# Norms of a one-layer hybrid decoder step: the sums of squares taken as columns of tokens, the last norm read from PSUM

## The chip, the cores and the metric

The kernel runs on one core of one Trainium2 chip. The metric is the device time of one execution in microseconds (us). Before the change it is 2406.41 us, the median of three runs (2404.97 to 2407.44).

## The reference, cut to what matters

One layer of a decoder with 512 prompt tokens and 32 sample tokens (eight sequences of four), D_MODEL = 2048, D_FF = 5632, all in float32:

```
def rmsnorm(x, w):
    y = xf * lax.rsqrt(jnp.mean(xf * xf, axis=-1, keepdims=True) + EPS)
    return (y * w.astype(jnp.float32)).astype(x.dtype)
...
h = rmsnorm(x, norm_mix_w);  proj = h @ w_in
...                                   # differential attention, and a Mamba-2 scan
y = y * jax.nn.silu(z)
y = rmsnorm(y.reshape(b, s, SSD_GROUPS, D_SSD // SSD_GROUPS), ...)
x = x + jnp.concatenate([att, y], axis=-1) @ w_out
hf = rmsnorm(x, norm_ffn_w);  g = hf @ w_gate;  u = hf @ w_up
...                                   # causal conv of width 3 on g
x = x + (jax.nn.silu(g_c) * u) @ w_down
y_prompt = rmsnorm(xp, norm_final_w);  y_sample = rmsnorm(xs, norm_final_w)
```

The norms that matter here are the first one, one for each of the two groups of the scan's output, the one ahead of the gated MLP, and the last one. There is also a small norm for each attention head, which the change leaves as it is.

## The kernel before, in words

Activations lie with features on the 128 partitions and tokens along the free dimension: 544 tokens in two halves of 272 (`HT`; in each half 256 prompt and 16 sample tokens). Weights stream from HBM in tiles of 128x1024, and each is split into a high and a low part (`whi` by ScalarE, `wlo` by VectorE), so that a product is three passes of TensorE over 272 columns (`mm3`, line 166). These products write the tiles `po`; there are nearly twelve thousand of them in the projections alone, and they fill the kernel.

TensorE's instructions run in exactly the order in which the code issues them. The other engines are put in order by a scheduler, except for a short stretch at the start of the MLP where the code's order holds for them too. Side work (attention, the scan, norms) consists of Python generators held by the class `Side` (line 61). After each `mm3` the generators whose time has come are resumed; `yield 5.0` asks to be resumed when TensorE has been given 5 us of further work by the planner's count. `side.finish(cond)` (line 89) doesn't wait for that count: it resumes generators at once until the condition holds, and puts no products in between.

A sum of squares over 2048 (or 512) features is built as a tile `sq` of 128x544 by ScalarE and VectorE or GpSimd. The sum over the partitions is a product with a 128x128 tile of ones, which leaves the same sum on every partition: one float32 product per half, 272 columns wide, into a tile `pn` (line 212). In the trace each float32 product is two instructions. ScalarE takes the square root of 128x272 values from `pn`, VectorE the reciprocal.

The places of these norms, by the names that the rest of the text uses:

- **norm1**: the first norm, at `k == 13` of the first products (line 281, helper `rms_rstd`, line 207). The following `podt` products and the evacuations of `xbc` use it.
- **gate0**: the norm of group 0 of the scan (line 622). It comes in the middle of the second `ssd` generator, ahead of the last small products of that generator, `pys` (line 598). Then `mixy[0]` is scaled and written to DRAM (`mixd`, line 626), and so is `mixy[1]` (`yd`, line 683). After it the pool `sS` is released. The first tiles of the next pool, `sT`, wait for every earlier user of that memory: the copy `q<-po` (line 728) waits for all these DMAs, and TensorE waits for the copy, which frees its `po` buffers.
- **gate1**: the norm of group 1 (line 1046), at the start of the output projection.
- **scaled**: a first scale of the residual for the MLP's input, from two of its sixteen tiles (line 1204).
- **norm2**: the norm ahead of the MLP (line 1315). Its result replaces the scale from `scaled`; the first evacuation of the gate branch asks for it by `side.finish` (line 303).
- **final0**, **final1**: the last norm, for each half of the tokens (`final`, line 1469). Half 0 runs beside the last products of half 1. Half 1 is the end of the kernel: 16 products of 128x272 on VectorE (10) and GpSimd (6), and the writes of `yT`.

The constants come in packs (`PACKS`, line 49). Each is one DMA.

Of the kernel before, what the change touches and what calls it, by code (L numbers as in the profile page):

```python
# [9 lines left out]
F32 = mybir.dt.float32  # L10
# [6 lines left out]
P = 128  # L17
# [31 lines left out]
PACKS = {  # L49
    "k0": [("nw_mix", P, NK), ("epsc", P, 1)],  # L50
    "k1": [("ones", P, P), ("nw_ffn", P, NK), ("nw_fin", P, NK)],
    "kS": [("conv_ssd", P, NC_X * (CW + 1)), ("prev_ssd", P, NC_X * DB * 3), ("dt_bias", P, SH), ("a_log", P, SH),
           ("d_skip", P, 8), ("maskT", P, P), ("tri", P, P), ("tri32", NS, NS3), ("blk32", NS, NS3),
           ("mask32", NS, NS), ("bmask", NS3, DB), ("ii", 2 * SH, SH), ("ii32", 2 * NS, NS), ("w_dt", P, NK * SH)],
    "kT": [("ident", P, P), ("nw_ssd", P, 8), ("cos", P, TOK), ("sin", P, TOK), ("cmask", P, P), ("smask", P, NS), ("sel", P, 64), ("isel", P, 64),
           ("csgn", P, 2), ("hmask", P, 2), ("dmask", P, 8), ("subw", P, 1), ("lamv", 64, 4)],
# [43 lines left out]
def body(tc, i, o):  # L100
# [105 lines left out]

    def rms_rstd(pool, sq, n, **kw):

        r = pool.tile([P, 2, HT], F32, name="rstd", **kw)
        for hf in range(2):  # L210
            pt = ps.tile([P, 512], F32, name="pn", tag=("sA", "pb")[hf])
            mm(pt[:, 0:HT], ones, sq[:, hf, :])
            A.activation(r[:, hf], pt[:, 0:HT], AF.Sqrt, scale=1.0 / n, bias=epsc)
            V.reciprocal(r[:, hf], r[:, hf])
        return r


    k0 = pack(cst, "k0")
    nw_mix, epsc = k0["nw_mix"], k0["epsc"]
    sK = tc.alloc_tile_pool(name="sK", bufs=1)  # L220
    kT = {}
    sC = tc.alloc_tile_pool(name="sC", bufs=1)
    sA = tc.alloc_tile_pool(name="sA", bufs=1)
    xs = {}
# [37 lines left out]
    k1 = pack(cst, "k1")  # L262
    ones, nw_ffn, nw_fin = (k1[n] for n in ("ones", "nw_ffn", "nw_fin"))
    V.tensor_tensor(ssq, ssq, ssq2, op=ALU.add)
    kS = pack(sC, "kS")
    kT.update(pack(sK, "kT"))
    ident, nssd = kT["ident"], kT["nw_ssd"]
    cpar = kS["conv_ssd"].rearrange("p (j t) -> p j t", t=CW + 1)
# [7 lines left out]
    for k in range(NK):  # L276
        for f in range(2):
            for hf in range(2):
                mm3(first[f][hf], kslice(fw[f], k), xs[k], hf, k == 0, k == NK - 1)
        if k == 13:  # L280
            rstd = rms_rstd(cst, ssq, DM, tag="rstd")
    sA.release()
# [335 lines left out]
    def gate0():  # L618
        my = mixy[0]
        while not squared:  # L620
            yield 0.7
        r = rms_rstd(sS, sq, 512, tag="spre", bufs=2)
        with tc.high_priority(offset=60):
            for j in range(4):
                V.scalar_tensor_tensor(my[:, j], my[:, j], nssd[:, j:j + 1], r, op0=ALU.mult, op1=ALU.mult)
                dma(out=mixd[8 + j], in_=my[:, j])
# [417 lines left out]
    def gate1():  # L1044
        yield 3.5
        rg = rms_rstd(sT, sq, 512, tag="pss")
        for j in range(4):
            n = 10 + j
            V.scalar_tensor_tensor(ys[j], ys[j], nssd[:, 4 + j:5 + j], rg, op0=ALU.mult, op1=ALU.mult)
            ms[n] = xslot(n)  # L1050
            A.activation(ms[n][0], ys[j], AF.Copy)
            V.tensor_tensor(ms[n][1], ys[j], rd(ms[n][0]), op=ALU.subtract)
# [149 lines left out]
    def scaled(x, s):  # L1202
        yield 6.5
        scale.append(rms_rstd(cst, ssq, 2 * P, tag="rstd"))
        for m in range(2):
            feed(m, x[m])
# [304 lines left out]
def host_inputs(x):  # L1511
# [132 lines left out]
```

## Time and profile before

| | |
|---|---|
| median of three runs | 2406.41 us |
| profiled execution, its own time | 2406.29 us |
| span in that profile (first to last instruction) | 2404.5 us |
| TensorE busy | 2342.6 us, 97% |
| VectorE busy | 1961.7 us, 82% |
| mean granted TensorE clock | 0.989 of full speed |

The profile comes from one execution. What an execution takes beyond its span (2406.29 - 2404.5 = 1.8 us) lies around the first and the last instruction. The share of busy time says which engine is used most; what a place costs is read from the idle time of TensorE there, and from what ended it.

### The profile page before, as it was taken

The numbers are of one execution on the slowest core, as the hardware profiler recorded it, in microseconds if no ns is written. First come the engines' busy times: TensorE is split into PE (matmuls) and PEld (weight loads), VectorE is DVE, ScalarE is ACT, GpSimd is POOL, SyncE is SP. The second block draws the span as 40 slices with busy tenths as digits, with TensorE's granted clock in tenths as the row PEclk, the third lists the DMA queues.
The fourth block names the chain that finished last, engine by engine and source line by source line (L and its number), as shares of the span: only waits on it lengthen the run. The fifth ranks groups of instructions, "written<-read, shape, count | busy, mean of one in ns | idle before, by whom it ended". The sixth has DMA issues, their size and how long they took to land.

```text
span 2404.5 us, 46378 instructions
## 1 busy us (share of the span) xinstructions
PE 2342.6 (97%) x18184; PEld 2294.0 (95%) x18184; DVE 1961.7 (82%) x2677; ACT 1200.5 (50%) x1917; POOL 612.4 (25%) x619
## 2 busy tenths in 40 slices
PE   7999989999999999999999999999999999999997
PEld 7999989999999999999999999999999899999996
DVE  8686779887877556988988888898888978878876
ACT  5645336666575333554444445444444644545455
POOL 4253233332321111222222222222221111211213
PEclk9999999999999999999999999999999999999998
DMA  4444444545454443334334343433433755747432
GB/s 159 133 125 140 147 161 145 165 151 165 160 170 151 157 140 118 123 124 139 119 123 135 110 141 125 140 118 121 136 110 132 225 183 178 231 154 253 122 123 75
DMA packets 172285, 350.44 MB, mean 146 GB/s; under 512 B 19474, under 2 KB 89874, under 8 KB 172066
## 3 DMA queue, kind: packets, MB, share of 16 engines
q1 hardware_dynamic: 168370, 335.51, 44.0%
q0 software_dynamic: 2880, 11.14, 1.1%
q8 instruction: 142, 2.33, 0.4%
q10 hardware_dynamic: 816, 0.84, 0.1%
q14 instruction: 77, 0.63, 0.1%
HBM read 293.07 MB, written 54.35 MB: 144 GB/s over the span
## 4 chain that ended last, share of the span: by engine, by line
PE 83%; DVE 9%; DMA 3%; issue 3%; ACT 2%; POOL 0%; SPq 0%; DVEq 0%; ACTq 0%; POOLq 0%
PE po L158 76%; PE scs L158 1%; DMA st<-hTs 1%; DVE xl L1083 1%; DVE wlo L1083 1%; PE pos L158 1%; DVE wx L1083 1%; PE sc L158 1%; DMA wraw<-in_w_last 1%; DVE wlo L151 1%; PE pys L158 1%; PE pvo L158 1%; PE py L158 0%; DMA xr<-in_xT 0%; DVE ssq L1501 0%
## 5 line engine op out<-in xcount | busy, mean ns | idle before, releaser
L158 PE MATMUL po<-xh,whi 128*128 128x272 f32 x3968 | 1158.1, 292 | 17.6 <-DVE q L728 6.3
L158 PE MATMUL po<-xh,wlo 128*128 128x272 f32 x3968 | 1150.1, 290 | 7.6 <-DVE wlo L151 4.3
L158 PE MATMUL po<-xl,whi 128*128 128x272 f32 x3968 | 1149.2, 290 | 4.7 <-DVE xl L254 4.5
L158 PEld LDWEIGHTS po<-xh,whi 128*128 128x128 f32 x3968 | 755.0, 190 | 25.8 <-issue 10.2
L158 PEld LDWEIGHTS po<-xh,wlo 128*128 128x128 f32 x3968 | 753.3, 190 | 14.5 <-DVE wlo L151 6.2
L158 PEld LDWEIGHTS po<-xl,whi 128*128 128x128 f32 x3968 | 754.0, 190 | 6.2 <-DVE xl L254 5.8
L1083 DVE TENSOR_TENSOR wlo<-wx,whi 128x1024 fp32r<-128x1024 f32 (+2 forms) x340 | 423.6, 1247 | 96.8 <-ACT whi L1089 94.2
L1089 ACT ACTIVATE whi<-wx 128x1024 fp32r<-128x1024 f32 (+2 forms) x340 | 342.1, 1006 | 293.0 <-PE po L158 272.3
L1162 ACT ACTIVATE u<-po 128x272 f32<-128x272 f32 x272 | 106.8, 393 | 317.3 <-PE po L158 317.3
L151 DVE TENSOR_TENSOR wlo<-wraw,whi 128x1024 fp32r<-128x1024 f32 (+1 forms) x132 | 168.2, 1279 | 52.4 <-ACT whi L150 52.1
L1083 DVE TENSOR_TENSOR wx<-wraw,wx 128x1024 f32<-128x1024 f32 (+2 forms) x136 | 189.9, 1397 | 4.5 <-DMA wraw<-in_w_down 1.4
L1083 DVE TENSOR_TENSOR wlo<-wraw,whi 128x1024 fp32r<-128x1024 f32 (+2 forms) x136 | 160.0, 1176 | 17.9 <-ACT whi L1089 17.8
L150 ACT ACTIVATE whi<-wraw 128x1024 fp32r<-128x1024 f32 (+1 forms) x132 | 127.7, 975 | 87.9 <-PE po L158 62.5
L158 PE MATMUL po<-T1h,wlo 128*128 128x272 f32 x512 | 148.1, 289 | 5.8 <-DVE wlo L1083 5.8
L158 PE MATMUL po<-T2h,whi 128*128 128x272 f32 x512 | 147.8, 289 | 4.2 <-ACT whi L1089 2.6
L158 PE MATMUL po<-T2h,wlo 128*128 128x272 f32 x512 | 148.4, 290 | 1.2 <-DVE wlo L1083 1.2
L158 PE MATMUL po<-B11h,wlo 128*128 128x272 f32 x512 | 147.8, 289 | 0.8 <-DVE wlo L1083 0.8
L158 PE MATMUL po<-T2l,whi 128*128 128x272 f32 x512 | 148.1, 289 | 0.0
L158 PE MATMUL po<-B11l,whi 128*128 128x272 f32 x512 | 147.6, 288 | 0.0
L158 PE MATMUL po<-T1l,whi 128*128 128x272 f32 x512 | 147.5, 288 | 0.0
L158 PE MATMUL po<-T1h,whi 128*128 128x272 f32 x512 | 147.2, 288 | 0.1
L158 PE MATMUL po<-B11h,whi 128*128 128x272 f32 x512 | 147.0, 287 | 0.0
(408 smaller groups left out, 4000.7 us busy)
## 6 DMA issues: line engine op xcount, KB each, us to landing
wx<-in_w_gu SPq DMA_DIRECT2D x88, 512.0 KB, 3.9
wraw<-in_w_gu SPq DMA_DIRECT2D x88, 512.0 KB, 4.2
wraw<-in_w_in SPq DMA_DIRECT2D x84, 512.0 KB, 3.9
kv<-in_kc SPq DMA_DIRECT2D x128, 128.0 KB, 2.6
kv<-in_vc SPq DMA_DIRECT2D x128, 128.0 KB, 2.8
wraw<-in_w_out SPq DMA_DIRECT2D x32, 512.0 KB, 4.1
wx<-in_w_down SPq DMA_DIRECT2D x32, 448.0 KB, 4.4
wraw<-in_w_down SPq DMA_DIRECT2D x32, 448.0 KB, 4.1
```

The source lines that it names most:

```text
L150: A.activation(hi[:, c], raw[:, c], AF.Copy)
L151: V.tensor_tensor(lo[:, c], raw[:, c], rd(hi[:, c]), op=ALU.subtract)
L158: T.matmul(out, lhsT=lhsT, rhs=rhs, start=start, stop=stop, skip_group_check=more)
L1083: e.tensor_tensor(out, a, b, op=op)
L1089: A.activation(h, src, AF.Copy)
L1162: A.activation(to, po, AF.Copy)
```

## The change

Instead of a product with a tile of ones on the stationary side, the squares are now the stationary operand (128 features by 128 tokens) and a column of ones (`one`, 128x4) streams past them. The result has tokens on the partitions: three columns per half, for tokens 0 to 127, 128 to 255 and 144 to 271 (the last overlaps, so that it is full). Square root and reciprocal then work on 128x6 values. To bring the result back, each column is broadcast as a stationary operand of 128x128 and multiplied with the identity (128, 128 and 16 columns), which leaves the row of tokens on every partition. ScalarE copies that from PSUM. A norm of both halves so has six products of 4 columns and six of 128 or 16, in place of two of 272. Between the two parts the generator yields 2.0 us. norm2 multiplies the small columns (`root`, kept from `scaled`) where it multiplied 128x272 tiles, and yields 4.0 instead of 5.0 ahead of its first part. In `final` VectorE multiplies by the row straight from PSUM, GpSimd by the copy. `ident`, `epsc` and `one` move into the pack that comes early, `ones` into the later one, and the first pack into a pool that is released sooner.

```diff
 PACKS = {
-    "k0": [("nw_mix", P, NK), ("epsc", P, 1)],
-    "k1": [("ones", P, P), ("nw_ffn", P, NK), ("nw_fin", P, NK)],
+    "k0": [("nw_mix", P, NK)],
+    "k1": [("ident", P, P), ("epsc", P, 1), ("one", P, 4), ("nw_ffn", P, NK), ("nw_fin", P, NK)],
...
-    def rms_rstd(pool, sq, n, **kw):
-        r = pool.tile([P, 2, HT], F32, name="rstd", **kw)
+    COLS = (0, P, HT - P)
+    def col_sums(parts, n, name):
+        pc = ps.tile([P, 8, 64], F32, name="pn", tag="sA")
+        for j, sqs in enumerate(parts):
+            for e, a in enumerate(COLS):
+                for m, sq in enumerate(sqs):
+                    mm(pc[:, 3 * j + e, 0:4], sq[:, a:a + P], one, m == 0, m == len(sqs) - 1)
+        k = 3 * len(parts)
+        c = cst.tile([P, 6], F32, name=name, tag=name)
+        A.activation(c[:, 0:k], pc[:, 0:k, 0], AF.Sqrt, scale=1.0 / n, bias=epsc)
+        return c
+    def col_spread(c, j, tag):
+        pt = ps.tile([P, 512], F32, name="pn", tag=tag)
+        for e, a in enumerate(COLS):
+            w = (P, P, HT - 2 * P)[e]
+            mm(pt[:, e * P:e * P + w], c[:, 3 * j + e:3 * j + e + 1].broadcast_to([P, P]), ident[:, P - w:P])
+        return pt[:, 0:HT]
+    def rms_rstd(r, sq, n):
+        c = col_sums([[sq[:, hf]] for hf in range(2)], n, "cols")
+        V.reciprocal(c, c)
+        yield 2.0
         for hf in range(2):
-            pt = ps.tile([P, 512], F32, name="pn", tag=("sA", "pb")[hf])
-            mm(pt[:, 0:HT], ones, sq[:, hf, :])
-            A.activation(r[:, hf], pt[:, 0:HT], AF.Sqrt, scale=1.0 / n, bias=epsc)
-            V.reciprocal(r[:, hf], r[:, hf])
-        return r
+            A.activation(r[:, hf], col_spread(c, hf, ("sA", "pb")[hf]), AF.Copy)
...
         if k == 13:
-            rstd = rms_rstd(cst, ssq, DM, tag="rstd")
+            rstd = cst.tile([P, 2, HT], F32, name="rstd", tag="rstd")
+            n1 = rms_rstd(rstd, ssq, DM)
+            next(n1)
+        if k == 15:
+            next(n1, None)
...
     def norm2():
         r2 = rstd_now[0] = scale[0]
-        yield 5.0
+        yield 4.0
+        c = col_sums([[ssq[:, hf]] for hf in range(2)], DM, "cols")
+        V.reciprocal(c, c)
+        V.tensor_tensor(c, c, u["root"], op=ALU.mult)
+        yield 2.0
         for hf in range(2):
-            pt = ps.tile([P, 512], F32, name="pn", tag=("sA", "pb")[hf])
-            mm(pt[:, 0:HT], ones, ssq[:, hf, :])
-            A.activation(ssq[:, hf], pt[:, 0:HT], AF.Sqrt, scale=1.0 / DM, bias=epsc)
-            V.tensor_tensor(ssq[:, hf], ssq[:, hf], r2[:, hf], op=ALU.mult)
-            V.reciprocal(r2[:, hf], ssq[:, hf])
+            A.activation(r2[:, hf], col_spread(c, hf, ("sA", "pb")[hf]), AF.Copy)
...
-        pt = ps.tile([P, 512], F32, name="pn", tag="sA")
-        for n, s in enumerate((ssq[:, hf], uc[(NK - 1) % 3])[:hf + 1]):
-            mm(pt[:, 0:HT], ones, s, n == 0, n == hf)
+        c = col_sums([[ssq[:, hf], uc[(NK - 1) % 3]][:hf + 1]], DM, "cols")
+        V.reciprocal(c[:, 0:3], c[:, 0:3])
+        if hf == 0:
+            yield 2.0
+        pt = col_spread(c, 0, "pb")
         r = sD.tile([P, 2, HT], F32, name="st", tag="st", bufs=5)[:, 0]
-        A.activation(r, pt[:, 0:HT], AF.Sqrt, scale=1.0 / DM, bias=epsc)
-        V.reciprocal(r, r)
+        A.activation(r, pt, AF.Copy)
...
-                e.tensor_tensor(y[:, n], x1[m + n][:, hf], r, op=ALU.mult)
+                e.tensor_tensor(y[:, n], x1[m + n][:, hf], r if e is G else pt, op=ALU.mult)
```

gate0 and gate1 run the new generator by `yield from rms_rstd(...)`; `scaled` has the same two parts, with the yield of 2.0 between them.

TensorE at norm2, before. `pn` is the tile of the sums; the first `po` rows end the product B21 of the MLP's first block, those behind it begin T3:

```order
L158 MATMUL po<-xh_11223,whi 128x272
L158 MATMUL po<-xh_11223,wlo 128x272
L158 MATMUL po<-xl_11224,whi 128x272
L158 MATMUL pn<-ssq_9609,k_288 128x272 x2
L158 MATMUL po<-xh_11291,whi 128x272
L158 MATMUL po<-xh_11291,wlo 128x272
L158 MATMUL po<-xl_11292,whi 128x272
```

The same place now; `cols` is the tile of 128x6 that VectorE finishes:

```order
L158 MATMUL po<-xh_11272,whi 128x272
L158 MATMUL po<-xh_11272,wlo 128x272
L158 MATMUL po<-xl_11273,whi 128x272
L158 MATMUL pn<-k_288,ssq_9645 128x4 x6
L158 MATMUL pn<-k_288,cols 128x128 x2
L158 MATMUL pn<-k_288,cols 128x16
L158 MATMUL po<-xh_11340,whi 128x272
```

A third row of `cols` for half 1 (two of 128 columns and one of 16, as above) stands ahead of the last row and is left out here because it repeats. The first part stands at the same product as before, and the second part follows it with no `po` row between.

VectorE at norm2, before. `wlo<-wx` splits the weights that come next, `pre<-u` is the evacuation that uses the norm:

```order
L1083 TENSOR_TENSOR xl_11454<-kp_9616,xh_11453 128x544
L1083 TENSOR_TENSOR wlo<-wx,whi 128x1024 x2
L1322 TENSOR_TENSOR ssq_9609<-ssq_9609,rstd 128x272 x2
L1323 RECIPROCAL rstd<-ssq_9609 128x272 x2
L305 TENSOR_TENSOR pre<-u_9602,rstd 128x256
L306 TENSOR_TENSOR pre<-u_9602,rstd 128x4x4
```

VectorE there now:

```order
L1110 TENSOR_TENSOR xl_11503<-kp_9652,xh_11502 128x544
L1110 TENSOR_TENSOR wlo<-wx,whi 128x1024 x2
L1354 RECIPROCAL cols<-cols 128x6
L1110 TENSOR_TENSOR wx<-wx 128x1024
L1355 TENSOR_TENSOR cols<-cols,root 128x6
L1110 TENSOR_TENSOR wx<-wx,wraw 128x1024
L1110 TENSOR_TENSOR wx<-wraw,wx 128x1024
L330 TENSOR_TENSOR pre<-u_9638,rstd 128x256
```

The small reciprocal stands behind the same two splits as the large one did, and a sum of 128x1024 stands between it and the product that TensorE needs.

VectorE at gate0, before. `mixy_504` is group 1, which needs the products `pys`, and `mixy_503` group 0, which needs the norm:

```order
L601 SCALAR_TENSOR_TENSOR mixy_504<-xss,kS,pys 128x2x16 x4
L214 RECIPROCAL rstd<-rstd 128x272 x2
L151 TENSOR_TENSOR wlo<-wraw,whi 128x1024
L625 SCALAR_TENSOR_TENSOR mixy_503<-mixy_503,kT,rstd 128x544 x4
L728 COPY q<-po 128x272 x2
```

VectorE there now (`mixy_516` is group 1, `mixy_515` group 0):

```order
L234 RECIPROCAL cols<-cols 128x6
L151 TENSOR_TENSOR wlo<-wraw,whi 128x1024
L651 SCALAR_TENSOR_TENSOR mixy_515<-mixy_515,kT,rstdg 128x544 x4
L626 SCALAR_TENSOR_TENSOR mixy_516<-xss,kS,pys 128x2x16 x4
L754 COPY q<-po 128x272 x2
```

The scaling of group 0 and its four writes now stand ahead of what needs `pys`. On TensorE 18 `po` products that stand between the two parts of the norm have moved ahead of `pys`, and the writes of `yd` go out after those of `mixd`.

## Rows read from the trace of the kernel before

**Rows 1.** The page's first part (busy time of each engine, its share of the span, its instructions) and its fourth (the chain of work that ended last, as shares of the span by engine).

```profile
PE 2342.6 (97%) x18184; PEld 2294.0 (95%) x18184; DVE 1961.7 (82%) x2677; ACT 1200.5 (50%) x1917; POOL 612.4 (25%) x619
...
PE 83%; DVE 9%; DMA 3%; issue 3%; ACT 2%; POOL 0%; SPq 0%; DVEq 0%; ACTq 0%; POOLq 0%
```

**Rows 2.** The timeline of TensorE (PE) at the first half of gate0: start in us, duration in us, line, operation, output and inputs, count. Products overlap, so that the distance of two starts is what one takes.

```profile
292.92 0.29 PE L158 MATMUL po<-xh,wlo 128*128 128x272 f32 x1
293.05 0.29 PE L158 MATMUL po<-xl,whi 128*128 128x272 f32 x1
293.17 1.08 PE L158 MATMUL pn<-gsq,k 128*128 128x272 f32 x4
294.18 0.30 PE L158 MATMUL pys<-ms,xdts 32*64 32x32 f32 x2
```

**Rows 3.** The same view at two small sums of the scan, of 16 columns.

```profile
58.76 1.23 PE L158 MATMUL pd<-kS,dtr 32*128 32x16 f32 x10
59.92 0.39 PE L158 MATMUL po<-xh,whi 128*128 128x272 f32 x1
```

**Rows 4.** Groups of instructions by line and operation: form and count, then busy time and mean ns of one, then the engine's idle time before them. The first two are of VectorE (DVE), the third, of the page's fifth part, is of ScalarE (ACT).

```profile
L214 DVE RECIPROCAL rstd<-rstd 128x272 f32<-128x272 f32 x8 | 14.4, 1829 | 4.2 <-ACT rstd L213 4.2
...
L805 DVE RECIPROCAL sm<-sm 128x2 f32<-128x2 f32 x32 | 5.0, 156 | 8.0 <-ACT p L804 7.9
...
L1162 ACT ACTIVATE u<-po 128x272 f32<-128x272 f32 x272 | 106.8, 393 | 317.3 <-PE po L158 317.3
```

**Rows 5.** Stretches of time: in each the busy time and the instructions of the five engines in the order PE, PEld, DVE, ACT, POOL, then the granted clock of TensorE as a share of full speed, the DMA's share and GB/s.

```profile
42.00:44.00 2.00, 2.00 (x12) 1.69 (x11) 0.51 (x1) 1.03 (x3) 0.00 (x0) 0.79 0.27 111
311.00:316.00 5.00, 5.00 (x23) 5.00 (x24) 2.72 (x7) 1.35 (x3) 4.89 (x7) 0.51 0.78 233
975.00:980.00 5.00, 5.00 (x31) 5.00 (x30) 5.00 (x6) 1.48 (x3) 0.34 (x3) 0.69 0.52 174
```

**Rows 6.** Timelines at gate0: the row that TensorE resumes with (in brackets its idle time before, and what ended it), then VectorE, and the queue of SyncE (SPq) with the writes of `mixd`; last, from the view of the tile `mixd`, for those four writes the time from issue to landing.

```profile
310.84 0.56 PE L158 MATMUL po<-xh,whi 128*128 128x272 f32 x1 [6.33 <-DVE q L728]
...
297.93 0.72 DVE L601 SCALAR_TENSOR_TENSOR mixy<-xss,kS,pys 128x32 f32<-128x32 f32 x4 [8.05 <-PE pys L158]
298.57 3.56 DVE L214 RECIPROCAL rstd<-rstd 128x272 f32<-128x272 f32 x2
...
303.12 2.86 DVE L625 SCALAR_TENSOR_TENSOR mixy<-mixy,kT,rstd 128x544 f32<-128x544 f32 x4
...
310.25 0.79 DVE L728 COPY q<-po 128x272 f32<-128x272 f32 x2 [3.13 <-DMA mixd<-mixy]
...
303.92 2.70 SPq L626 DMA_DIRECT2D mixd<-mixy  x4
...
DMA to landing us min/median/max: 4.0/4.0/4.4
```

**Rows 7.** Timelines at gate1 (VectorE) and at scaled (TensorE).

```profile
772.25 0.28 DVE L756 SCALAR_TENSOR_TENSOR obs<-obs,kT,orr 128x64 f32<-128x64 f32 x1
...
779.69 1.35 DVE L1033 TENSOR_TENSOR xl<-mt,xh 128x544 fp32r<-128x544 f32 x2
...
802.49 0.39 PE L158 MATMUL po<-xh,wlo 128*128 128x272 f32 x1 [0.35 <-DVE wlo L151]
```

**Rows 8.** Timelines at norm2: TensorE, then VectorE, then TensorE some microseconds later.

```profile
970.36 1.18 PE L158 MATMUL pn<-ssq,k 128*128 128x272 f32 x4
973.30 0.39 PE L158 MATMUL po<-xh,whi 128*128 128x272 f32 x1 [1.76 <-ACT u L1162]
...
972.20 2.62 DVE L1083 TENSOR_TENSOR xl<-kp,xh 128x544 fp32r<-128x544 f32 x4
974.74 2.35 DVE L1083 TENSOR_TENSOR wlo<-wx,whi 128x1024 fp32r<-128x1024 f32 x2
977.01 0.78 DVE L1322 TENSOR_TENSOR ssq<-ssq,rstd 128x272 f32<-128x272 f32 x2
977.71 3.55 DVE L1323 RECIPROCAL rstd<-ssq 128x272 f32<-128x272 f32 x2
...
984.22 1.21 DVE L1083 TENSOR_TENSOR wx<-wx 128x1024 f32<-128x1024 f32 x1
...
988.48 0.39 PE L158 MATMUL po<-T1h,wlo 128*128 128x272 f32 x1 [1.21 <-DVE wlo L1083]
```

**Rows 9.** Timelines at the end of the kernel: VectorE while half 0's last norm and its products run beside TensorE's, then TensorE, ScalarE, VectorE and GpSimd (POOL) at the last norm of half 1.

```profile
2369.45 1.85 DVE L1478 RECIPROCAL st<-st 128x272 f32<-128x272 f32 x1 [0.88 <-ACT st L1477]
...
2375.05 0.43 DVE L1494 TENSOR_TENSOR x<-x,po 128x272 f32<-128x272 f32 x1
2375.98 0.82 DVE L1501 TENSOR_TENSOR ssq<-ssq,u 128x272 f32<-128x272 f32 x1 [0.50 <-ACT u L1499]
...
2389.86 0.72 PE L158 MATMUL pn<-u,k 128*128 128x272 f32 x2
...
2390.68 0.49 ACT L1477 ACTIVATE st<-pn,k 128x272 f32<-128x272 f32 x1 [0.32 <-PE pn L158]
...
2391.20 1.85 DVE L1478 RECIPROCAL st<-st 128x272 f32<-128x272 f32 x1 [1.86 <-ACT st L1477]
...
2393.45 6.63 DVE L1483 TENSOR_TENSOR y<-x,st 128x272 f32<-128x272 f32 x9
...
2393.13 5.59 POOL L1483 TENSOR_TENSOR y<-x,st 128x272 f32<-128x272 f32 x6 [8.29 <-DVE st L1478]
```

More of the change, by code (lines that the diff above doesn't have):

```diff
@@ L54 @@
            ("mask32", NS, NS), ("bmask", NS3, DB), ("ii", 2 * SH, SH), ("ii32", 2 * NS, NS), ("w_dt", P, NK * SH)],
-    "kT": [("ident", P, P), ("nw_ssd", P, 8), ("cos", P, TOK), ("sin", P, TOK), ("cmask", P, P), ("smask", P, NS), ("sel", P, 64), ("isel", P, 64),
+    "kT": [("ones", P, P), ("nw_ssd", P, 8), ("cos", P, TOK), ("sin", P, TOK), ("cmask", P, P), ("smask", P, NS), ("sel", P, 64), ("isel", P, 64),
            ("csgn", P, 2), ("hmask", P, 2), ("dmask", P, 8), ("subw", P, 1), ("lamv", 64, 4)],
@@ L205, in xslot @@
         return [xsp.tile([P, 2, HT], FR, name=f"x{n}{k}", tag=f"x{n}{k}") for n in "hl"]
-    def rms_rstd(pool, sq, n, **kw):
-        r = pool.tile([P, 2, HT], F32, name="rstd", **kw)
-        for hf in range(2):
-            pt = ps.tile([P, 512], F32, name="pn", tag=("sA", "pb")[hf])
-            mm(pt[:, 0:HT], ones, sq[:, hf, :])
-            A.activation(r[:, hf], pt[:, 0:HT], AF.Sqrt, scale=1.0 / n, bias=epsc)
-            V.reciprocal(r[:, hf], r[:, hf])
-        return r
-    k0 = pack(cst, "k0")
-    nw_mix, epsc = k0["nw_mix"], k0["epsc"]
+    COLS = (0, P, HT - P)
[19 more added lines that the diff above has]
+        yield 2.0
+        for hf in range(2):
+            A.activation(r[:, hf], col_spread(c, hf, ("sA", "pb")[hf]), AF.Copy)
     sK = tc.alloc_tile_pool(name="sK", bufs=1)
@@ L222, in body @@
     sC = tc.alloc_tile_pool(name="sC", bufs=1)
+    nw_mix = pack(sC, "k0")["nw_mix"]
     sA = tc.alloc_tile_pool(name="sA", bufs=1)
@@ L262, in body @@
     k1 = pack(cst, "k1")
-    ones, nw_ffn, nw_fin = (k1[n] for n in ("ones", "nw_ffn", "nw_fin"))
+    ident, epsc, one, nw_ffn, nw_fin = (k1[n] for n in ("ident", "epsc", "one", "nw_ffn", "nw_fin"))
     V.tensor_tensor(ssq, ssq, ssq2, op=ALU.add)
@@ L266, in body @@
     kT.update(pack(sK, "kT"))
-    ident, nssd = kT["ident"], kT["nw_ssd"]
+    ones, nssd = kT["ones"], kT["nw_ssd"]
     cpar = kS["conv_ssd"].rearrange("p (j t) -> p j t", t=CW + 1)
@@ L621, in gate0 @@
             yield 0.7
-        r = rms_rstd(sS, sq, 512, tag="spre", bufs=2)
+        r = sS.tile([P, 2, HT], F32, name="rstdg", tag="spre", bufs=2)
+        yield from rms_rstd(r, sq, 512)
         with tc.high_priority(offset=60):
@@ L1045, in gate1 @@
         yield 3.5
-        rg = rms_rstd(sT, sq, 512, tag="pss")
+        rg = sT.tile([P, 2, HT], F32, name="rstdg", tag="pss")
+        yield from rms_rstd(rg, sq, 512)
         for j in range(4):
@@ L1203, in scaled @@
         yield 6.5
-        scale.append(rms_rstd(cst, ssq, 2 * P, tag="rstd"))
+        c = col_sums([[ssq[:, hf]] for hf in range(2)], 2 * P, "root")
+        u["root"] = c
+        d = cst.tile([P, 6], F32, name="cols", tag="cols")
+        V.reciprocal(d, c)
+        yield 2.0
+        r = cst.tile([P, 2, HT], F32, name="rstd", tag="rstd")
+        for hf in range(2):
+            A.activation(r[:, hf], col_spread(d, hf, ("sA", "pb")[hf]), AF.Copy)
+        scale.append(r)
         for m in range(2):
@@ L1472, in final @@
             yield 3.0
-        pt = ps.tile([P, 512], F32, name="pn", tag="sA")
-        for n, s in enumerate((ssq[:, hf], uc[(NK - 1) % 3])[:hf + 1]):
-            mm(pt[:, 0:HT], ones, s, n == 0, n == hf)
+        c = col_sums([[ssq[:, hf], uc[(NK - 1) % 3]][:hf + 1]], DM, "cols")
+        V.reciprocal(c[:, 0:3], c[:, 0:3])
+        if hf == 0:
+            yield 2.0
+        pt = col_spread(c, 0, "pb")
         r = sD.tile([P, 2, HT], F32, name="st", tag="st", bufs=5)[:, 0]
-        A.activation(r, pt[:, 0:HT], AF.Sqrt, scale=1.0 / DM, bias=epsc)
-        V.reciprocal(r, r)
+        A.activation(r, pt, AF.Copy)
         for m in range(0, NK, 2):
@@ L1561, in host_inputs @@
     c["ones"] = np.ones((P, P), fl)
+    c["one"] = np.ones((P, 4), fl)
     c["tri"] = (ar(P)[:, None] <= ar(P)[None, :]).astype(fl)
```

## Prediction

> **What bounds the kernel now.** I read the engines' busy time first: TensorE works for 97% of the span, VectorE for 82%, and TensorE holds 83% of the chain that ended last, VectorE 9% [rows 1]. So an instruction added to TensorE's stream lengthens the run by its own duration, unless TensorE idles there, and one taken from VectorE is worth something only where TensorE waits for VectorE. I therefore went through TensorE's idle time place by place, and at each norm read what ended it. Four places matter: 6.33 us at gate0, 0.35 at scaled, 1.76 at norm2 with 1.21 soon behind it, and the end of the kernel, where TensorE is done [rows 6 to 9]. The stretches of granted clock came last: where TensorE has idled, it goes on at a lower clock for a while (311 to 316 us: 0.51, which is 1.2 GHz) [rows 5].
>
> **What a norm costs TensorE.** The old pair: four instructions of 272 columns from 293.17 to 294.18, 1.01 us, 0.25 each [rows 2]. The new pair: six products of 4 columns and six of 128 or 16, two instructions each, 24. None of before has these shapes. The nearest row is ten instructions of 16 columns from 58.76 to 59.92: 0.116 each [rows 3]. Bounds: by columns alone, 0.25 x 128/272 = 0.12 for a wide one and nearly nothing for a narrow one, so 1.06 for the pair; from above, 0.25 for every one, 6.0. I take 0.116, as the nearest shape: 24 x 0.116 = 2.78, so +1.77 a pair, +0.89 for half a norm.
>
> The Trainium skill, page "TensorE: Matmul & The Clock Gate", section "Back-to-back issue gap", gives small products an issue floor of about 25 ns, by which the narrow ones would be nearly free; its section on loading the stationary operand says that the load lasts by its columns, about P/1.2 ns, 107 ns for 128, whatever streams after it. The 116 ns of [rows 3] agree with the second rule.
>
> **What it takes from VectorE.** Twelve reciprocals of 1.83 us become seven small ones of about 0.16 (as the 128x2 form) [rows 4]: 12 x 1.83 - 7 x 0.16 = 20.8 us. ScalarE copies where it took square roots, at about 0.39 (as `u<-po`) [rows 4]: no change.
>
> **norm1.** +1.77 at full clock; from 42 to 44 us it is 0.79 [rows 5], giving 2.2. I take +2.0 (1.8 to 3.4, if the burst halves the clock). The later scale is hidden by the `podt` products.
>
> **gate0.** Before, VectorE waited for `pys` until 297.93, and only then came group 0's reciprocals (3.56) and its scaling from 303.12; the writes of `mixd` left from 303.92 to 306.62, took 4.0 to land, and VectorE's copy of `q`, which waits for them, ran at 310.25, TensorE from 310.84 [rows 6]. Now the norm's second part ends 2.78 us of products and 18 `po` products (0.125 each, 2.25) after 293.17, at about 298.2; two copies bring it to 299.0, group 0 is scaled by 301.9. `pys` is late by 1.77 + 2.25, so VectorE does group 1 at 301.95 to 302.7, and the last `yd` write leaves by about 303.9. With 4.0 to land, `q` starts at about 308.0, TensorE at 308.6: -2.2. TensorE's own work, which ended at 310.84 - 6.33 = 304.5, ends at 306.3, so 2.3 us of idle remain. Their lower clock costs less: before, 5 us at 0.51 lose 2.5; behind the 1.76 of idle at norm2, 5 us at 0.69 lose 1.5 [rows 5, 8]. I take -1.5, as the remaining idle may be shorter. Sum -3.7. Bounds: all idle and all lost clock return, -6.33 - 2.5 + 1.77 = -7.1; or writes land as late as before, 0.
>
> **gate1.** +1.77. Besides, the order of the changed program puts the scaling of `obs` and the `mixd` and `mt` transfers that follow behind two weight loads and a split; before, `obs` ran at 772.25 and the `xl` that needs it at 779.69 [rows 7], about 3 us before its product. They come some 4 us later: +0.8. Sum +2.6 (1.8 to 4).
>
> **scaled.** +1.77, less the 0.35 that VectorE caused [rows 7]: +1.4 (1.4 to 1.8).
>
> **norm2, the largest term.** Before, TensorE did four instructions at 970.36 and went on at 973.30; the scale was ready only at 981.2, and nothing on TensorE needed it before [rows 8]. Now `side.finish` puts the second part directly behind the first, so TensorE itself waits for VectorE's result with all later products queued behind. VectorE has `xl` x4 (972.20, 2.62) and `wlo` x2 (974.74, 2.35) ahead of it, until 977.01 [rows 8]. Then: small reciprocal 0.16, the sum `wx` that stands next, 1.21 [rows 8], the small product, taken like the reciprocal at 0.16: 978.55. Twelve products of 0.116 end at 980.0, at half clock 981.3; I take 980.6. That is 7.3 after 973.30. VectorE is then ahead by what its reciprocals took, and the gap of 1.21 at 988.48 goes: +6.1. The lost clock of 975 to 980 was there before [rows 5] and counts no second time. Bounds: 980.0 and a clock loss smaller by 1.0 give 4.5; 981.3 with the later gap kept, and a further 0.5 of clock, 8.5. Who waits: every product behind it; ScalarE and VectorE run on into full buffers.
>
> **final0.** +0.89 on TensorE, against a reciprocal of 1.85 on VectorE (2369.45), whose `ssq` sums take 0.82 instead of 0.44 while GpSimd works [rows 9]. From here the two engines feed each other: 0 (-0.3 to +0.9).
>
> **The end.** `pn<-u` started at 2389.86, the square root at 2390.68, the reciprocal at 2391.20 (1.85), nine products from 2393.45 (6.63, 0.74 each, beside GpSimd's six, 5.59) [rows 9]; so VectorE ended at 2400.1, and 4.4 us later the span. Now: ten small instructions after the last square, 2391.1; square root 0.2, reciprocal 0.16, six small products 0.7: 2392.4. VectorE's ten products read PSUM; the row that does so beside GpSimd is `x<-x,po` with 0.43, while `ssq` with two SBUF inputs takes 0.82 [rows 9]. At 0.38 to 0.43 they end by 2396.7. GpSimd starts after the copy, about 2393.0, and with 0.93 each, as before, ends at 2398.6, or at 2397.5 if the neighbour no longer slows it: -1.9 (-2.6 to -0.5).
>
> The Trainium skill, "SBUF — State Buffer", section "Who interferes with whom", lets only the port pair that VectorE and GpSimd share cause contention. The 0.43 beside 0.82 agrees.
>
> **Sum.** +2.0 - 3.7 + 2.6 + 1.4 + 6.1 + 0 - 1.9 = +6.5 us, on the profiled 2406.29 us: 2412.8 us. That execution lies 0.12 under the median, so the base needs no correction. The terms' bounds, taken together with some cancelling, give this case 2408.5 to 2417.
>
> **Rivals.** *norm2 doesn't stall.* If VectorE, freed earlier, has done `xl` and `wlo` before the sums arrive, norm2 costs 1.77 - 1.21 = +0.6: 2407.3 us. Against it: these stand behind `kp`, which needs the evacuation of products that TensorE has just made, and VectorE is busy without a gap from 972.20 [rows 8]. *The clock falls at each burst.* If norm1, gate1, scaled and final0 lose what 975 to 980 lost, 1.5 each: +6.0, 2418.8 us. For it speaks the 0.79 at norm1, against it that the old bursts there were hardly shorter. *The other side: VectorE's queue is the hidden bound.* Each reciprocal stands in order ahead of a `wlo` or `xl` that TensorE needs soon; if all the freed 20.8 us return against 5 x 1.77 + 2 x 0.89 = 10.7 added, the time is 2396.2 us, and the change gains from the point where 51% of the freed time lay on the path. Against it: the gaps that VectorE ended beside norms sum to 0.35 + 1.21 outside gate0. *Small products cost by their columns.* Then four pairs (norm1, gate1, scaled, norm2; at gate0 transfers set the end) cost 0.05 instead of 1.77: -6.9, 2405.9 us. Against it stands [rows 3]. The first rule of the page on TensorE, above, would lead here.
>
> **Chances.** Forecast 0.58, norm2 without a stall 0.17, clock 0.10, VectorE as the bound 0.09, columns 0.06. About 0.2% (4.8 us) is what a measurement of this kernel tells from no change: under 2401.6 is faster, over 2411.2 slower. Faster: VectorE 0.09 and 0.02 from a gate0 that returns everything, 0.11. Same: columns 0.06, norm2 0.15, and 0.12 of the forecast's own lower part, 0.33. Slower: 0.56. For 8 in 10 the range must reach down over the second and fourth rivals and up to the clock's: 2403.0 to 2418.5.
>
> **What would show it.** Right: TensorE idle some 7 us behind the `pn` of norm2, ended by `cols` of VectorE; 24 small instructions at about 0.116; TensorE resuming at gate0 at 308 to 309 with yd writes as the last wait; the last VectorE product by 2397. Wrong: narrow products far below 0.1 us; no gap at norm2; less TensorE idle in places that have no norm; `q` waiting as long as before.

## The result and the profile after

The changed kernel takes 2421.86 us, the median of four runs (2420.38 to 2422.96); the kernel before takes 2406.93 us beside it (2404.97 to 2408.42, four runs). The ratio is 1.0051, with a 95% interval of 1.0035 to 1.0066, which is 12 us; the two medians alone lie 14.9 us apart. The change makes the kernel slower, as forecast, but by about twice as much as forecast, and the time lies above the range.

The profiled execution has a span of 2420.7 us, 16.2 more than before. The page's first part answers to [rows 1]:

```profile
PE 2353.2 (97%) x18308; PEld 2306.0 (95%) x18308; DVE 1939.5 (80%) x2671; ACT 1202.3 (50%) x1924; POOL 610.7 (25%) x619
```

VectorE has lost 22.2 us of work (1961.7 to 1939.5), and TensorE, the bound, has gained 10.6. What TensorE waited for, longest first, is the view that shows more than this (us in total, times, the longest):

```profile
PE po L158 <- DVE wlo L1110: 9.5, 12, 1.7
PE po L158 <- ACT u L1189: 8.9, 5, 2.6
PE po L158 <- ACT whi L150: 7.3, 2, 5.2
PE pn L158 <- DVE cols L1355: 6.6, 1, 6.6
PE po L158 <- DVE xl L275: 5.7, 3, 2.2
PE po L158 <- DVE wlo L151: 3.0, 4, 1.0
PE po L158 <- DVE q L754: 2.8, 1, 2.8
...
PE po L158 <- DVE kp L1256: 2.0, 1, 2.0
```

The wait for `q` shrank from 6.33 us [rows 6] to 2.8. Of the waits of 2 us and more, three are new: one of 6.6 us for `cols`, one of 2.0 for `kp`, and a second one for `whi` (7.3 in two; the longest, 5.2, is the start of the kernel).

To see where the 16.2 us lie, I counted the `po` products along TensorE's timeline (each of the three passes of an `mm3` counts as one). Their number is the same in both kernels, so the time between the same two products can be compared. `again` is a second profile of the same program, from a run told of below.

| stretch (by its norm) | before | before, again | after | after, again | forecast | after - before |
|---|---|---|---|---|---|---|
| start and norm1 | 49.98 | 49.89 | 51.72 | 52.42 | +2.0 | +1.7 |
| gate0, 300 products around it | 56.43 | 56.65 | 58.82 | 57.54 | -3.7 | +2.4 |
| gate1, 200 products | 26.68 | 27.02 | 32.51 | 33.83 | +2.6 | +5.8 |
| scaled, 80 products | 10.89 | 10.89 | 12.66 | 12.68 | +1.4 | +1.8 |
| norm2, 150 products | 25.06 | 25.04 | 31.27 | 30.44 | +6.1 | +6.2 |
| late MLP, no norm in it | 363.2 | 364.3 | 366.3 | 364.6 | 0 | +3.1 |
| last 46 products to the end | 22.75 | 22.81 | 20.89 | 21.63 | -1.9 | -1.9 |

The rows add up to +19.1; the rest, -2.9, lies in the stretches left out (between norm1 and gate0, -1.3: a stretch of lowered clock near 200 us that this profile of the changed kernel lacks and the other three have; where `w_last` is loaded, -1.4, of which below), so a single difference of under 2 us in this table says little. The small products themselves came out as taken from [rows 3]: TensorE's timeline after, at gate0, has 12 instructions from 297.14 to 298.48, 0.112 each.

```profile
297.14 1.41 PE L158 MATMUL pn<-k,cols 128*128 128x128 f32 x12
298.48 0.30 PE L158 MATMUL pys<-ms,xdts 32*64 32x32 f32 x2
```

**norm2** is as it was worked out. VectorE after, then TensorE:

```profile
984.36 2.35 DVE L1110 TENSOR_TENSOR wlo<-wx,whi 128x1024 fp32r<-128x1024 f32 x2
986.63 0.18 DVE L1354 RECIPROCAL cols<-cols 128x6 f32<-128x6 f32 x1
986.73 1.18 DVE L1110 TENSOR_TENSOR wx<-wx 128x1024 f32<-128x1024 f32 x1
987.83 0.15 DVE L1355 TENSOR_TENSOR cols<-cols,root 128x6 f32<-128x6 f32 x1
...
988.13 2.71 PE L158 MATMUL pn<-k,cols 128*128 128x128 f32 x12 [6.59 <-DVE cols L1355]
```

The reciprocal stands behind the splits as before [rows 8], `wx` between it and the small product, and TensorE is idle for 6.59 us; then it runs its twelve products at half clock (2.71 instead of 1.41).

**gate1.** VectorE, the SyncE queue, ScalarE, and the rows at which TensorE waited:

```profile
779.77 0.28 DVE L782 SCALAR_TENSOR_TENSOR obs<-obs,kT,orr 128x64 f32<-128x64 f32 x1
...
780.31 2.39 SPq L999 DMA_DIRECT2D mixd<-obs  x2
...
787.91 1.32 ACT L1058 ACTIVATE xh<-mt 128x544 fp32r<-128x544 f32 x2 [7.82 <-DMA mt<-mixd]
791.68 2.00 ACT L150 ACTIVATE whi<-wraw 128x1024 fp32r<-128x1024 f32 x2 [2.45 <-PE po L158]
...
792.77 1.23 DVE L151 TENSOR_TENSOR wlo<-wraw,whi 128x1024 fp32r<-128x1024 f32 x1 [2.79 <-ACT whi L150]
793.91 0.78 DVE L1256 TENSOR_TENSOR kp<-po,xr 128x272 f32<-128x272 f32 x2
...
788.62 0.39 PE L158 MATMUL po<-xh,whi 128*128 128x272 f32 x1 [1.04 <-ACT xh L1058]
...
794.40 0.39 PE L158 MATMUL po<-xh,whi 128*128 128x272 f32 x1 [2.01 <-DVE kp L1256]
```

`obs` is scaled at 779.77 instead of 772.25 [rows 7], 7.5 us later. By 2.7 of these the whole changed kernel is behind here (the norm's first product starts at 767.21 instead of 764.49), so `obs` itself is 4.8 late. The two transfers behind it end at 787.9: from `obs` to the `xh` that needs them it is 8.1 us instead of 4.9 (772.25 to 777.13). So the operand comes 8.1 us later, counted from the norm, and the products that need it wait.

**gate0.** VectorE, ScalarE, the SyncE queue and TensorE, answering to [rows 6]; the last two rows are two of the kernel before, VectorE's and ScalarE's:

```profile
302.71 0.72 DVE L626 SCALAR_TENSOR_TENSOR mixy<-xss,kS,pys 128x32 f32<-128x32 f32 x4 [0.64 <-PE pys L158]
308.85 1.22 DVE L151 TENSOR_TENSOR wlo<-wraw,whi 128x1024 fp32r<-128x1024 f32 x1 [5.42 <-ACT whi L150]
309.99 0.78 DVE L754 COPY q<-po 128x272 f32<-128x272 f32 x2
...
307.76 1.06 ACT L150 ACTIVATE whi<-wraw 128x1024 fp32r<-128x1024 f32 x1 [8.78 <-PE po L158]
316.83 2.67 ACT L739 ACTIVATE kvh<-kv 128x512 fp32r<-128x512 f32 x4 [8.01 <-DMA kv<-in_kc]
...
328.31 2.00 ACT L150 ACTIVATE whi<-wraw 128x1024 fp32r<-128x1024 f32 x2
...
302.98 2.78 SPq L709 DMA_DIRECT2D yd<-mixy  x4
310.10 0.33 SPq L149 DMA_DIRECT2D wraw<-in_w_in  x1
310.95 12.09 SPq L907 DMA_DIRECT2D kv<-in_kc  x18
...
310.48 0.39 PE L158 MATMUL po<-xh,whi 128*128 128x272 f32 x1 [2.75 <-DVE q L754]
329.42 0.39 PE L158 MATMUL po<-xh,whi 128*128 128x272 f32 x1 [2.17 <-ACT whi L150]
...
305.90 1.22 DVE L151 TENSOR_TENSOR wlo<-wraw,whi 128x1024 fp32r<-128x1024 f32 x1
...
327.06 2.01 ACT L150 ACTIVATE whi<-wraw 128x1024 fp32r<-128x1024 f32 x2
```

VectorE scaled group 1 at 302.71, 0.8 later than forecast, and the four `yd` writes took 2.78 us to issue, so that the last left at 305.76, not by 303.9. It had landed by 308.5, 3.5 us after the start of its issue and only 0.6 later than forecast. But `q` stands behind a `wlo` (308.85), which waits for `whi` (307.76), which waits for a buffer that TensorE's own products hold. The order of VectorE's rows shown ahead of the prediction leaves this `wlo` out, in both kernels; before, it ran at 305.90, while the writes were still under way, and cost nothing. TensorE ended its own products at 307.73 (310.48 - 2.75), not at 306.3: from 300 to 308 us the clock is 0.58, where before 298 to 304 had 0.72:

```profile
300.00:308.00 8.00, 7.72 (x41) 6.90 (x40) 2.79 (x7) 0.24 (x1) 0.00 (x0) 0.58 0.94 344
```

So TensorE resumes at 310.48, only 0.36 earlier than before (0.74 counted from the norm's first product, 293.56 and 293.17), and 19 us later it waits 2.17 for a `whi`. That `whi` starts at 328.31, where before it started at 327.06.

**The end.** VectorE and GpSimd, answering to [rows 9]:

```profile
2410.46 3.21 DVE L1519 TENSOR_TENSOR y<-x,pn 128x272 f32<-128x272 f32 x9
...
2410.15 4.35 POOL L1519 TENSOR_TENSOR y<-x,st 128x272 f32<-128x272 f32 x6 [8.69 <-ACT st L1514]
```

VectorE's nine products take 3.21 us instead of 6.63 and GpSimd's six 4.35 instead of 5.59. From the last addition `x<-x,po` (2388.91 and 2405.89) to the end of the span it is 15.6 before and 14.8 after: 0.8 us. The other 1.1 of the table's last row I put down to VectorE being less behind TensorE there (half 0's reciprocal is gone; run 7 below, which keeps it, lacks this gain); against them, half 0's norm costs TensorE 0.9 us a little earlier (100 products there take 13.89 us instead of 13.02).

### The profile page after: what moved, and what is told of

Read it like the earlier page. It is cut to its first block, busy times and chain, and to the rows that moved or that the text cites. A ratio compares the mean times of both kernels' runs of the same rounds, so it can differ in the third digit from the quotient of the medians.

```text
span 2420.7 us, 46625 instructions
## 1 busy us (share of the span) xinstructions
PE 2353.2 (97%) x18308; PEld 2306.0 (95%) x18308; DVE 1939.5 (80%) x2671; ACT 1202.3 (50%) x1924; POOL 610.7 (25%) x619
## 5 line engine op out<-in xcount | busy, mean ns | idle before, releaser
L158 PEld LDWEIGHTS po<-xh,wlo 128*128 128x128 f32 x3968 | 752.3, 190 | 13.1 <-DVE wlo L1110 4.8
L1110 DVE TENSOR_TENSOR wlo<-wraw,whi 128x1024 fp32r<-128x1024 f32 (+2 forms) x136 | 159.5, 1173 | 19.4 <-ACT whi L1116 19.3
```

The lines of the kernel that those rows point to most:

```text
L158: T.matmul(out, lhsT=lhsT, rhs=rhs, start=start, stop=stop, skip_group_check=more)
L1110: e.tensor_tensor(out, a, b, op=op)
```

## The experiments

Unless said otherwise, an edit is made in the changed kernel, and the ratio is to the kernel before, run beside it. In the old form, a norm has a product of 272 columns again, with `one` broadcast to 128 columns in the place of `ones`.

**1. VectorE's order at norm2.**

```diff
-        V.reciprocal(c, c)
-        V.tensor_tensor(c, c, u["root"], op=ALU.mult)
+        with tc.high_priority(offset=60):
+            V.reciprocal(c, c)
+            V.tensor_tensor(c, c, u["root"], op=ALU.mult)
```

> The changed kernel, with the small reciprocal and the small product of norm2 ahead of the splits xl and wlo in VectorE's order. Theory: TensorE's 6.59 us of idle at norm2 come from what stands ahead of these two on VectorE; it falls to 1 to 2 us, with it the lowered clock behind it, and the kernel is 5 to 6.5 us faster than the changed one (about 2416 us). Rival (the small products themselves and their hand-overs between engines cost the time): the idle stays over 4 us, and the time moves by less than 2 us.

Measured: 2418.05 us, ratio 1.0032 (1.0020 to 1.0045); the changed kernel itself has 1.0051 to 1.0054. VectorE and TensorE:

```profile
985.54 0.19 DVE L1355 RECIPROCAL cols<-cols 128x6 f32<-128x6 f32 x1 [0.96 <-ACT cols L220]
985.65 0.40 DVE L1369 TENSOR_TENSOR u<-po,u 128x272 f32<-128x272 f32 x1
985.96 0.16 DVE L1356 TENSOR_TENSOR cols<-cols,root 128x6 f32<-128x6 f32 x1
...
986.26 1.48 PE L158 MATMUL pn<-k,cols 128*128 128x128 f32 x12 [1.06 <-DVE cols L1356]
```

The idle falls from 6.59 to 1.06 us, and the norm2 stretch from 31.27 to 25.09 us (26.25 in run 6, which has the same edit); the kernel before takes 25.06. The products and hand-overs that the rival blamed are all still there, so the loss was VectorE's queue.

**2. norm2 in the old form.** `col_sums`, the spread and the two copies are replaced by the two products, square roots, products and reciprocals of before.

> The changed kernel with norm2 alone in the old form. Theory: the loss at norm2, 6.3 us in the alignment of the two traces, returns: about 2415.5 us, and norm2_prio comes within 1.5 us of it. Rival (a norm in the new form costs its 1.8 us of TensorE and little else, the rest of the loss is spread over the kernel): about 2420 us.

Measured: 2416.29 us, ratio 1.0023 (1.0011 to 1.0035), close to the forecast. Run 1 is 1.8 us slower, a little more than the 1.5 expected, but the two intervals overlap. The norm2 stretch takes 26.48 us.

**3. obs ahead in VectorE's order.**

```diff
-        V.reciprocal(r, r)
         with tc.high_priority(offset=60 if n == 64 else 0):
+            V.reciprocal(r, r)
             V.scalar_tensor_tensor(ob, ob, subw, r, op0=ALU.mult, op1=ALU.mult)
```

> The changed kernel, with the small reciprocal of the last sample heads (orr) ahead in VectorE's order, so that obs is scaled where it was before. Theory: of the 5.2 us lost at gate1, 1.77 are products and the rest comes from obs being 7.5 us late; the waits of 1.04, 0.24 and 2.01 us in front of the last steps of the output projection go, and the time falls by about 3.3 us, to 2418.5 us. Rival (these waits come from VectorE's or ScalarE's weights, not from obs): the waits stay, under 1 us of change.

Measured: 2417.39 us, ratio 1.0032 (1.0020 to 1.0044). `obs` is scaled in time again:

```profile
774.55 0.28 DVE L782 SCALAR_TENSOR_TENSOR obs<-obs,kT,orr 128x64 f32<-128x64 f32 x1
```

The waits for `xh`, `xl` and `kp` are gone, all three: the gate1 stretch takes 28.67 us, 1.7 to 2.0 more than before, which is the added products. The wait for `kp`, 6 us after the one for `xh`, belonged to it too: `kp` stands behind a `wlo` whose `whi` waits for products that had been late; in run 3 it stands ahead of that `wlo`, as before the change. (Run 8, with gate1 in the old form, has a wait for `kp` of 1.5 us too, without a `wlo` in front of it; why is open.)

**4. gate0 in the old form.**

> The changed kernel with gate0 alone in the old form. Theory from the two traces: gate0's new form lost 2.9 us on balance, since the 3.6 us of idle that it saved at 308 us came back as a lower clock and as a wait for whi at 329 us; so this kernel is about 3 us faster than the changed one, 2419 us. Rival, the step of the prediction: the new gate0 gains 3.7 us, and undoing it makes the kernel 2425.5 us.

Measured: 2419.66 us, ratio 1.0044 (1.0029 to 1.0058). The wait for `q` is 6.37 again and that for `whi` 0.44:

```profile
312.75 0.57 PE L158 MATMUL po<-xh,whi 128*128 128x272 f32 x1 [6.37 <-DVE q L762]
330.67 0.39 PE L158 MATMUL po<-xh,whi 128*128 128x272 f32 x1 [0.44 <-ACT whi L150]
```

Both numbers of mine were off: the gate0 stretch takes 57.03 us, 0.5 to 1.8 less than with the new form. Over all profiles of this study it takes 56.2 to 57.0 with the old form (five profiles) and 57.0 to 58.8 with the new (seven that keep gate0 as changed), about 1 us more, far from the gain of the prediction.

**5. The changed kernel once more, 6. both edits of order, and 7. the last norm alone.** Run 6 has the edits of runs 1 and 3. Run 7 has all norms in the old form but half 1 of the last one.

> The changed kernel once more, unchanged, on the chip of the other runs of this call, as their common base. Theory: the same places as in its first profile: 6 us at norm2, 4 us or more behind gate1, ratio to the kernel before about 1.005. Rival (a good part of the 15 us was that one execution or that chip): a ratio under 1.003.

> The changed kernel with both edits of VectorE's order, at norm2 and at obs. Theory: the two losses are separate and both return, 6 and 4 to 5 us, so that what is left over the kernel before is the added products (1.77 each at norm1, gate1, scaled, 1.1 at gate0) less what the end gives, 3 to 6 us: ratio 1.001 to 1.0025. Rival (the waits move to the next late producer when one is taken away): 1.003 or more.

> All norms in the old form but the last one (half 1), which is as in the changed kernel. VectorE's and TensorE's orders are those of the kernel before up to the last norm. Theory: the end gains 0.8 to 1.5 us (GpSimd's six products set it now, not VectorE's ten), ratio 0.9993 to 0.9997. Prediction's term: 1.9 us. Rival (the early packs or the pool of the first pack cost something): slower than the kernel before by over 2 us.

Measured: run 5 2425.69 us, ratio 1.0054 (1.0038 to 1.0071); run 6 2413.64 us, 1.0008 (0.9997 to 1.0019); run 7 2407.60 us, 0.9981 (0.9971 to 0.9991), beside 2411.64 us for the kernel before. The loss of the change is the program's, not one execution's. The two edits of order add up: together they take away 0.0046 of the 0.0054. Run 7 gains more than expected. Its trace shows 0.3 us at the end and 1.3 where `w_last` is loaded, some 55 us before it: there TensorE waits 1.0 to 1.1 us for VectorE's `x` in both profiles of the kernel before, and at most 0.4 in the eleven others, two of them with the old norms. What the eleven have in common are the moved packs, so I put this gain down to them and not to a norm. The first 200 products take 0.7 us less in run 7 and 1.1 less in run 8 than before. The rest of the ratio's 4.6 us (2.2 to 7 by the interval) I can't place.

**8. GpSimd takes four of the last sixteen products.** As run 7, with this edit:

```diff
-            e = G if hf == 0 or m in (4, 10, 14) else V
+            e = G if hf == 0 or m in (4, 10) else V
```

> As the run with the last norm alone, and GpSimd takes four of its sixteen products instead of six. Theory: GpSimd's six, 4.35 us and then a write, end the changed kernel; with four they end before VectorE's twelve, and the end comes 1 to 1.5 us earlier than with six, 2 to 3 us before that of the kernel before: ratio 0.9988 to 0.9992. Rival (the landing of the last writes sets the end, whoever makes them): no change against six.

Measured: 2406.56 us, ratio 0.9978 (0.9967 to 0.9988), the fastest version here, faster than both kernels; against run 7 no difference that the intervals can tell. VectorE's and GpSimd's products both end earlier than in the kernel before, and from the last addition to the end it is 14.6 us, against 15.3 in run 7 and 15.6 before. Of the 0.7 against run 7, 0.4 lie ahead of the sixteen products: from the start of VectorE's row of products to the end it is 10.0 us, 10.3 in run 7 and 11.1 before. The 1 to 1.5 us expected of four instead of six did not come; the rival, by which the writes set the end, is nearer.

**9. No yield between the parts of gate0.** `rms_rstd` gets an argument in place of the 2.0, and gate0 passes 0.0.

> The changed kernel with no yield between the two parts of gate0, so that fifteen of the po products that had moved ahead of pys stand behind it again; everything else on TensorE is as in the changed kernel. Theory: gate0's saved time was lost because pys, and with it the last writes and a wlo that the copy of q stands behind, came later by these products and by a lowered clock; TensorE resumes at q 1 to 2 us earlier against the start of the norm, the wait for whi some 20 us later shrinks from 2.2 to under 1 us, and the segment around gate0 takes 56 us or less instead of 57 to 58.8 (of 56.4 before). Rival (the landing of the writes sets the time, whatever TensorE does in between): the segment stays at 57 us or more.

Measured: 2424.12 us, ratio 1.0055 (1.0040 to 1.0070); the stretch takes 59.88 us, the wait for `q` is 3.35, that for `whi` 2.13. The expectation was wrong. VectorE shows why:

```profile
307.24 1.23 DVE L151 TENSOR_TENSOR wlo<-wraw,whi 128x1024 fp32r<-128x1024 f32 x1 [3.86 <-ACT whi L150]
308.39 0.56 DVE L626 SCALAR_TENSOR_TENSOR mixy<-xss,kS,pys 128x32 f32<-128x32 f32 x3
310.87 1.22 DVE L151 TENSOR_TENSOR wlo<-wraw,whi 128x1024 fp32r<-128x1024 f32 x1 [1.93 <-ACT whi L150]
312.60 0.79 DVE L754 COPY q<-po 128x272 f32<-128x272 f32 x2 [0.50 <-DMA yd<-mixy]
```

In the order that this edit gives, three of the four last scalings stand behind a `wlo` that waits for TensorE, so that the writes left later still. It doesn't isolate the step that it was meant for, but the same trap decides.

**10. The kernel before, profiled again.**

> The kernel before, profiled once more. It tells how far two profiles of one program differ place by place. Theory: the segments at gate1 (11.25 and 15.43 us), scaled (10.89) and norm2 (25.06) come back within 0.3 us but for stretches of lowered clock of 1.7 us each, while the late part (from the middle of the MLP) differs by 1 to 3 us, as much as the changed kernel seemed to lose there. Rival: the late part comes back within 0.5 us, so that the changed kernel's loss there is its own.

Measured: 2409.70 us, ratio 1.0003 (0.9990 to 1.0016). The stretches at the norms come back within 0.35 us (table above), the late MLP 1.1 us longer. The eight profiles with norm2 in the new form have 363.1 to 367.7 us there, 365.0 in the mean, the four profiles of before and of runs 7 and 8 have 362.0 to 364.3, 363.2 in the mean. A part of the changed kernel's late loss is chance; whether 1 to 2 us are its own stays open. Run 2, which has the rest of the change but norm2 in the old form, takes 361.9 there.

**11. The last products of VectorE from SBUF.**

```diff
-                e.tensor_tensor(y[:, n], x1[m + n][:, hf], r if e is G else pt, op=ALU.mult)
+                e.tensor_tensor(y[:, n], x1[m + n][:, hf], r, op=ALU.mult)
```

> The changed kernel with VectorE's last ten products reading the row from the copy in SBUF, as GpSimd's do. Theory: VectorE's products take 0.7 us each again beside GpSimd's (6.6 in place of 3.2 us for nine), but the writes of the last 2.2 MB run at full rate in both, so that the time from the last addition to the end grows by under 1 us from 14.8 us. Prediction's step (VectorE's products set the end): it grows by 2 us or more.

Measured: 2424.74 us, ratio 1.0063 (1.0043 to 1.0082). VectorE and GpSimd:

```profile
2411.78 6.63 DVE L1519 TENSOR_TENSOR y<-x,st 128x272 f32<-128x272 f32 x9
...
2411.46 5.59 POOL L1519 TENSOR_TENSOR y<-x,st 128x272 f32<-128x272 f32 x6 [9.31 <-ACT st L1514]
```

Reading the row from PSUM is what made both engines faster: with the copy, they take 6.63 and 5.59 us to the hundredth as before. Yet from the last addition to the end it is 16.3 us. That is 1.4 more than the 14.8 of the expectation, between its two sides; but 0.6 of this lie ahead of VectorE's products, where the last small products ran at half clock, as in run 5 (15.5 us). From the start of VectorE's row of products to the end it is 11.1 us with the copy and 10.3 with PSUM, so 0.8 of VectorE's 3.4 us reach the end. What sets the end shows in windows of 1 us of the changed kernel's last writes (the last three columns are clock, DMA share and GB/s):

```profile
2412.00:2413.00 1.00, 0.00 (x0) 0.00 (x0) 1.00 (x4) 0.00 (x0) 1.00 (x2) 0.50 1.03 338
2413.00:2414.00 1.00, 0.00 (x0) 0.00 (x0) 0.67 (x2) 0.00 (x0) 1.00 (x3) 0.50 1.03 341
2414.00:2415.00 1.00, 0.00 (x0) 0.00 (x0) 0.00 (x0) 0.00 (x0) 0.50 (x1) 0.50 1.01 338
```

The eight writes are 2.2 MB (16 x 128 x 272 x 4 bytes); at some 340 GB/s that is 6.5 us, whatever the engines do. In the kernel before, the DMA engines had gaps in between (0.61 to 1.01); now they have none.

## Why the prediction was right and wrong

The direction and its main cause were right. The price of a new pair (+1.77 at scaled and at gate1, once `obs` is out of the way), norm1 (from its first product to the 200th of the table 14.7 to 15.0 us in six of nine profiles, 13.0 in runs 7 and 8, so 1.7 to 2.0; 16.2 to 17.8 where a lowered clock falls on it) and norm2 (5.2 to 6.5 over the profiles, +6.1 forecast) are as worked out, and run 1 shows norm2's mechanism by taking it away. The rivals fell: VectorE as a hidden bound (22.2 us less work on it, and the kernel is slower; its 5 x 1.77 + 2 x 0.89 is 10.6, not 10.7, and nothing hangs on that), columns as the price (0.112 a piece), and no stall at norm2. The clock's rival holds in part: there are stretches of half clock behind norm2's stall, at gate0 and in most profiles behind gate1's waits, but none behind scaled, and over the whole kernel the mean granted clock is 0.991 and 0.987 in the two profiles of the changed kernel, 0.989 before.

Three steps failed.

- **gate0, -3.7 forecast, about +1 measured.** The step that failed is the end of the account: "-2.2" of idle and "-1.5" of clock count as saved once TensorE has gone on, and what TensorE waits for next was put at nothing. Counted from the norm's first product, TensorE was to go on at 15.4 us (308.6), against 17.7 before. In four of the seven profiles with this gate0 it does so at 15.7 to 15.9, nearly as forecast, in the other three at 16.7 to 16.9. But 19 us later it needs a `whi` of ScalarE, which starts 33.4 to 34.8 us after the norm's first product with this gate0 and 33.7 to 34.5 with the old one. So what was saved is waited out there: 1.3 to 2.2 us in all seven, at most 0.44 in the five profiles with the old gate0, and in five of the seven a stretch at half clock follows. The loads of `kv`, behind a weight load on SyncE's queue, seem to keep that `whi` where it was (first issued at 310.95 instead of 310.35, `kvh` at 316.83); this is read from the trace, and no run took that link away.

  The step "With 4.0 to land, `q` starts at about 308.0, TensorE at 308.6" failed as well, by less. I had taken the landing as the only wait of `q` and asked nothing of what stands ahead of it on VectorE, the `wlo` that by way of `whi` waits for TensorE. The idle time is 2.75 to 2.9 us in all seven profiles, and in the first it is this chain (1.06 for `whi`, 1.22 for `wlo`, the first `q`) from the end of TensorE's own products. These end 13.0 us after the norm's first product in the four profiles (forecast 13.1), and there the chain and the landing let `q` start at the same time; in the three others they end at 13.9 to 14.2, since a longer stretch at half clock falls on them, and the chain makes `q` some 1 us later than the landing would. No run took the `wlo` away.
- **gate1, +2.6 forecast, +5.8 and +6.8 in the two pairs of profiles.** The cause was the one named, `obs` late. The term "They come some 4 us later: +0.8" was mis-sized: `obs` is 4.8 us later, counted from the norm, but the transfers behind it take 3.2 us more, so that the operand is 8.1 late; its wait is 1.3 us (1.04 and 0.24), and there is a second wait of 2.0 for `kp` that I hadn't followed. Run 3 returns the whole excess.
- **The end, -1.9 forecast, -0.8 measured.** The products did what was forecast, 3.21 us for nine. The step "VectorE ended at 2400.1, and 4.4 us later the span" failed: I took the engines' last product as what ends the run, with a fixed time behind it. That time is 4.4 us before and in run 11, and 6.2 with the faster products: the writes, at some 340 GB/s, are then further behind the engines.

The three come to some 9 us over the forecast. With the late MLP's open 1 to 2 us, final0 (-0.2 measured, 0 forecast) and the 1.3 gained where `w_last` is loaded, which the prediction didn't have, +6.5 becomes about 16 us. That is the difference of the two profiles (16.2); the runs as a whole have 12 to 15, and which of the terms is smaller in them I can't say.

## What to carry to other kernels

Making a step short on an engine with slack gains nothing when the same edit puts a hand-over to that engine into the bottleneck engine's own order: the time that counts is how much work stands ahead of the short step in the other engine's queue. Where an idle time is to go, list everything ahead of the waiting instruction on its engine, not only the transfer it waits for, and look for a wait that leads back to the bottleneck engine itself. Then ask what the bottleneck engine waits for next: if that comes no earlier, the time saved is only waited out later. For the end of a kernel, divide the bytes of the last writes by the rate before any engine is made faster there.

## What the runs showed of the hardware that was not expected

- A second operand read from PSUM sped up both engines: VectorE's 128x272 product from 0.74 to 0.36 us and GpSimd's, which still reads SBUF alone, from 0.93 to 0.73 (run 11 puts both back). I had forecast the first from `x<-x,po` and only allowed for the second. The Trainium skill, "SBUF — State Buffer", section "Who interferes with whom", says that a VectorE instruction with two SBUF inputs contends with GpSimd's reads and one with a single SBUF input does not; run 11 agrees.
- TensorE's lowered clock came in stretches that each lost some 1.7 to 7 us, in places that differ from one profile to the next of the same program: near 200 us the changed kernel has one in its second profile and none in its first. The hundred products there take 19.3 and 16.6 us, and 17.9 in both profiles of the kernel before.
